# Inverse in tiles of 32 rows, attention scores of two heads together, and new rates for the work beside them

## The chip, the cores and the metric

The program runs on one core of one Trainium2 chip. The metric is the device time of one execution in microseconds (us); three executions of the kernel before took 1747.9, 1748.63 and 1761.38 us, median 1748.63.

A core has a matrix engine (TensorE, PE in the profile; its weight loads are PEld), VectorE (DVE), ScalarE (ACT), GpSimd (POOL) and SyncE (SP), which here issues DMA transfers. The engines run side by side, each through its own list of instructions in order, and wait for each other by semaphores. SBUF is the on-chip memory with 128 partitions, PSUM the small memory into which TensorE writes.

## The reference

All arrays are fp32, 256 tokens (T) of 1024 features (D). Two blocks run one after the other:

- `first_block`: two layers of attention with an mLSTM branch, each followed by a convolutional feed-forward network (FFN, 2816 wide).
- `second_block`: one layer. A mixer of three branches, each of which reads the tokens ("lat") and a second sequence of 256 context tokens ("ctx"): HGRN2, RWKV-7 and neighbourhood attention. Then a mixture of 32 experts, all of whose weights are read.

The change touches two of the branches. RWKV-7 is a recurrence over tokens, run forwards and backwards, for 4 heads of 64, first over ctx and then over lat:

```
def step(s, inp):
    r_t, w_t, k_t, v_t, kk_t, ak_t = inp
    sa = jnp.einsum('bhvk,bhk->bhv', s, kk_t)
    s = s * w_t[:, :, None, :] - sa[..., None] * ak_t[:, :, None, :] + v_t[..., None] * k_t[:, :, None, :]
    return s, jnp.einsum('bhvk,bhk->bhv', s, r_t)
```

The kernel does 64 tokens at once, and for that has to invert one unit triangular 64x64 matrix for each chunk of 64 tokens, head and direction. Neighbourhood attention (8 heads of 64) scores each token against the window of 4 rows by 16 columns around it, with a bias by relative place, and against all 256 context tokens, under one softmax:

```
s_win = jnp.where(in_win[:, :, None, :], s_win + bias, NEG_INF)
s_ctx = jnp.einsum('bhjqd,bhld->bhjql', q_row, kc_h) * scale
```

## The kernel before, in words

**Projections.** The state x stays in SBUF, features on partitions. Weights are streamed: `load` (L442) issues a DMA on SP into a `raw` tile; `split_w` makes two tiles of it, `hi` by a copy on ACT (L451) and `lo` by a subtraction on DVE (L453). Each product is three matmuls: `mm3` (L474 to L476, 256 tokens wide) or `mm3n` (L487 to L489, tokens as weights).

**Order of the work.** Code is written as Python generators. `background(gen, rate)` adds one to a list, and each `tick()` of the code in front adds `rate` to each entry's account and runs one step per whole number. So a rate of 0.6 means three steps in five ticks. From what is so recorded a scheduler makes each engine's list; the lists below show the result.

**RWKV-7.** `rwkv(rp, j, m, lat)` (L1296) treats two heads (j) and runs four times: the two ctx runs as background steps (rate 0.8) inside the two FFNs, about 345 to 430 us and 800 to 880 us, the two lat runs in `middle()`, about 1075 to 1245 us. One run is a preparation (from L1307: decay, keys `kt`, `at`, `kr`, five transposes by L644, the products L1402), then the inverse, then the steps over chunks. The inverse takes eight units side by side (4 chunks by 2 heads), each as two 64x64 matrices, one for each direction, on the two halves of the 128 partitions. It grows X = inverse of blocks of 2, 4, ... 64 rows in six levels (L1427). Level 0 is elementwise. At each of the other five, `bt` is the part of the matrix that joins two blocks (DVE, L1429); `products` (L1424) computes bt*X into PSUM with 16 matmuls 64x64; ACT copies it to y (L1436); `products` computes X*y; DVE subtracts it from X (L1439); DVE transposes X into XT in squares of 32 (L1440). At the last level XT itself is updated (L1443). A product waits for the copy or the transpose before it, so in PE's list other matmuls stand between.

**Neighbourhood attention.** `scores(hd)` (L1750), one head at a time: a DMA of the bias, 128x384 (L1754); a mask added to it on POOL (L1755); for each half of the queries (128 tokens) two matmuls of 256 columns into one PSUM buffer "d", window and context (L1759). Their 64 features lie on partitions 0 to 63 for even heads and 64 to 127 for odd ones. DVE adds the bias (L1763), ACT copies the context part (L1765), then come maximum, exponential, four transposes (L644) and the product with the values (L1786). Scores run two pieces ahead.

**`middle()`** (L1823) runs the mixer of the tokens: HGRN2 (`hg`) in front, with `rwkv_lat` (`rk`) beside it at 0.6; after that `na_inputs`, the projections of neighbourhood attention; then neighbourhood attention with the rest of `rk`, whose rate stays at 0.6. PSUM has two buffers "d", three "a", two "y", one "f". The expert stage begins at about 1313 us: 32 experts, whose weights (L2079, L2097) come by DMA straight into the matmuls.

Of the kernel before, what the change touches and what calls it, by code (L numbers as in the profile page):

```python
# [15 lines left out]
AF = mybir.ActivationFunctionType  # L16
OP = mybir.AluOpType
AX = mybir.AxisListType
PSUM = bass.MemoryType.PSUM
P = 128  # L20
T = 256
NEG = -1.0e30
# [14 lines left out]
ADA_RATE, RK_RATE, MID_RATES = (0.8, 0.45, 0.8, 0.45), 0.8, (0.6, 1.0, 1.0, 1.0, 0.6)  # L37
# [143 lines left out]
def _consts2():  # L181

    c = Vecs()
    t = np.arange(P)

    q = np.arange(T)
# [9 lines left out]
    k, c = c, Vecs()  # L196
    c.add("tri", np.concatenate([t[:, None] > t[None, :], t[:, None] < t[None, :]], axis=1))
    r, c = c, Vecs()
# [11 lines left out]
    for b in (1, 2, 4, 8, 16, 32):  # L210
        same = s // (2 * b) == u // (2 * b)
        lev.append(par(same & (s // b < u // b), same & (s // b > u // b)).reshape(P, -1))
    c.add("rklev", np.concatenate(lev, axis=1))
    c.add("eye2", np.tile(np.eye(64), (2, 1)))
    n, c = c, Vecs()

    qc, kc = t[:, None] % 64, np.arange(64)[None, :]
    w0 = np.clip(qc - 8, 0, 48)
    c.add("nawin", np.where((kc >= w0) & (kc < w0 + 16), 0.0, NEG))
    return k, r, e, n, c  # L220


def prep(inputs):
# [78 lines left out]
    a["rpb"] = np.stack(b).reshape(P, -1)  # L302
# [7 lines left out]
    for group, k in zip(("all", "one", "two", "tri", "moe", "rk", "na"), (*_consts(), *_consts2())):  # L310
        a["k_" + group] = k.array()
        cat.update({n: (group, *x) for n, x in k.at.items()})
# [39 lines left out]
class Net:  # L352
# [943 lines left out]
    def rwkv(self, rp, j, m, lat):  # L1296
# [117 lines left out]
        X, XT = ti([8, 64], "kt"), ti([8, 64], "at")  # L1414
# [3 lines left out]
        f3 = lambda t: t.rearrange("p (s c) -> p s c", s=8)  # L1418
        units = [(g, p, slice(64 * p, 64 * p + 64)) for g in range(8) for p in range(2)]

        def products(tag, l_, r_):
            ps = self.ps(tag)
            for g, p, r in units:
                nc.tensor.matmul(ps[r, g * 64 : g * 64 + 64], l_(g, p, r), r_(g, p, r), start=True, stop=True, skip_group_check=True)  # L1424
            return ps

        for l in range(6):  # L1427
            bt = ti([8, 64], "bt", 2)
            nc.vector.tensor_tensor(f2(bt), f2(AT), lev[:, l, :].unsqueeze(1).to_broadcast([P, 4, P]), OP.mult)  # L1429
            if l == 0:  # L1430
                nc.vector.scalar_tensor_tensor(XT, bt, -1.0, self.C("eye2").unsqueeze(1).to_broadcast([P, 8, 64]), OP.mult, OP.add)
                nc.vector.transpose(f1(X), f1(XT))
                continue
            ps = products("a", lambda g, p, r: bt[r, g, :], lambda g, p, r: X[r, g, :])
            y = ti([8, 64], "y1")
            nc.scalar.copy(f1(y), ps)  # L1436
            if l < 5:
                ps = products("a", lambda g, p, r: XT[r, g, :], lambda g, p, r: y[r, g, :])
                nc.vector.tensor_tensor(X, X, f3(ps), OP.subtract)  # L1439
                nc.vector.transpose(f1(XT), f1(X))  # L1440
            else:
                ps = products("a", lambda g, p, r: y[r, g, :], lambda g, p, r: XT[r, g, :])
                nc.vector.tensor_tensor(XT, XT, f3(ps), OP.subtract)  # L1443
            yield

# [299 lines left out]
    def neighbourhood(self, np_, m):  # L1745
# [4 lines left out]
        def scores(hd):  # L1750

            hs = slice(64 * (hd % 2), 64 * (hd % 2) + 64)
            bias = self.two("twoa").rearrange("p a t -> p (a t)")[:, :384].rearrange("p (x c) -> p x c", c=64)
            nc.sync.dma_start(bias, self.A["rpb"][:, hd * 384 : hd * 384 + 384].rearrange("p (x c) -> p x c", c=64))  # L1754
            nc.gpsimd.tensor_tensor(bias, bias, self.C("nawin").unsqueeze(1).to_broadcast([P, 6, 64]), OP.add)  # L1755
            for i in range(2):
                ps = self.ps("d")
                for n, k in enumerate((kl[hd // 2][hs], self.naK[hs, hd // 2, :])):
                    nc.tensor.matmul(ps[:, n * T : n * T + T], q[hd // 2][hs, i * P : i * P + P], k, start=True, stop=True,  # L1759
                                     skip_group_check=True)  # L1760
                s = self.tmp(512, "nas")
                b0 = 2 * (1 - i)
                nc.vector.tensor_tensor(s[:, :T].rearrange("p (r c) -> p r c", c=64), ps[:, :T].rearrange("p (r c) -> p r c", c=64),  # L1763
                                        bias[:, b0 : b0 + 4, :], OP.add)
                nc.scalar.copy(s[:, T:], ps[:, T:])  # L1765
                mx = self.tmp(1, "namx", bufs=4)
                nc.vector.tensor_reduce(mx, s, AX.X, OP.max)
                nc.vector.tensor_scalar(mx, mx, -1.0, None, OP.mult)
                nc.scalar.activation(s, s, AF.Exp, bias=mx, accum_out=den[:, i, hd : hd + 1])
                yield s  # L1770

        todo = [(hd, i) for hd in range(8) for i in range(2)]
        ready = (s for hd in range(8) for s in scores(hd))
# [49 lines left out]
    def middle(self):  # L1823
        nc, x = self.nc, self.x
        self.ew = {"ew0": self.ectx.enter_context(self.pool("ew0"))}
        with self.pool("yp") as yp, self.pool("mid") as mp, self.phase("s", {256: 3, 512: MID_BUFS}):
# [6 lines left out]
            self.consts("na", mp)  # L1833
# [18 lines left out]
            while na in self.bg:  # L1852
                self.tick()
            self.background(self.prefetch(5), OUT_RATES[2])
# [341 lines left out]
```

## Time and profile before

| what | value |
|---|---|
| executions | 1747.9, 1748.63, 1761.38 us |
| the profiled execution | 1758.49 us; span 1756.4 us |
| PE, DVE, ACT, POOL busy, share of the span | 90%, 64%, 43%, 4% |
| DMA, mean over the span | 262 GB/s |
| expert stage, 1313 to 1756 us | 443 us, DMA at 408 GB/s |

The profiled execution is 9.9 us above the median of the three. Shares of busy time are averages over stages with different limits. A "record" is one matmul instruction in the trace; each fp32 matmul of the inverse and of the scores leaves two records. `PE L1424 ... x32` in a timeline is a run of 32 records of one kind without another between: its start, and the time from the first's start to the last's end. A matmul's record is longer than the distance to the next one, since they are pipelined, so a run's cost is the distance of starts. "PEclk" is TensorE's granted clock, 1.00 for 2.4 GHz and 0.50 for 1.2 GHz.

### The profile page before, as it was taken

How to read it: one execution, taken by the hardware profiler on the slowest of the kernel's cores; microseconds unless marked ns; L12 is line 12 of the kernel's file. 1: busy time of each engine (PE TensorE's matmuls, PEld its weight loads, DVE VectorE, ACT ScalarE, POOL GpSimd, SP SyncE). 2: the span in 40 equal slices, each digit the busy share in tenths (PEclk: the TensorE clock that was granted, in tenths of full speed). 3: DMA queues.
4: the chain of work that ended last, by engine and by line, in shares of the span. 5: the costliest groups of instructions: out<-in, count | busy, mean ns of one | idle time of the engine just before them, and what ended most of it. 6: DMA issues, size and time to landing. Idle time of an engine off the chain costs nothing.

```text
span 1756.4 us, 32561 instructions
## 1 busy us (share of the span) xinstructions
PE 1576.2 (90%) x13542; PEld 1271.6 (72%) x13542; DVE 1118.8 (64%) x2155; ACT 758.8 (43%) x1259; POOL 72.8 (4%) x77
## 2 busy tenths in 40 slices
PE   4999999999998999999999999999989777776776
PEld 4898999899997899989999899878874312221211
DVE  7989868898897887789889878666652111111011
ACT  3576545764455754556455576553431000000000
POOL 0000000020010000001011001001000000000000
PEclk8899999999999999999999999989989888988878
DMA  9745765666675467466567733223459999999998
GB/s 392 310 159 209 262 246 192 223 216 236 226 263 190 179 247 281 172 230 239 194 224 259 281 138 132 74 76 138 195 212 419 419 416 416 417 417 418 419 416 343
DMA packets 76809, 460.81 MB, mean 262 GB/s; under 512 B 8562, under 2 KB 11122, under 8 KB 28146
## 3 DMA queue, kind: packets, MB, share of 16 engines
q1 hardware_dynamic: 74352, 452.45, 67.1%
q10 hardware_dynamic: 2306, 6.24, 1.0%
q8 instruction: 108, 1.77, 0.4%
q14 instruction: 43, 0.35, 0.1%
HBM read 457.61 MB, written 1.05 MB: 261 GB/s over the span
## 4 chain that ended last, share of the span: by engine, by line
PE 57%; DMA 24%; DVE 12%; ACT 4%; issue 3%; SPq 0%; POOL 0%; DVEq 0%; ACTq 0%; POOLq 0%
DMA ew<-in_wgu 11%; PE d L474 9%; PE d L476 9%; PE d L475 9%; DMA ew<-in_wdown 8%; DVE lo L453 4%; PE y L474 3%; PE y L476 3%; PE y L475 3%; PE a L1424 3%; DVE raw L537 3%; PE d L2079 2%; DMA raw<-in_ws 2%; PE a L2008 1%; ACT hi L451 1%
## 5 line engine op out<-in xcount | busy, mean ns | idle before, releaser
L451 ACT CAST hi<-raw 128x1024 fp32r<-128x1024 f32 x309 | 322.7, 1048 | 295.6 <-PE d L475 173.1
L453 DVE TENSOR_TENSOR lo<-raw,hi 128x1024 fp32r<-128x1024 f32 x309 | 379.9, 1236 | 86.2 <-ACT hi L451 84.8
L474 PE MATMUL d<-hhi,hi 128*128 128x256 f32 x1320 | 387.4, 295 | 13.7 <-ACT hhi L608 10.4
L475 PE MATMUL d<-hlo,hi 128*128 128x256 f32 x1320 | 382.4, 290 | 3.7 <-DVE hlo L611 3.2
L476 PE MATMUL d<-hhi,lo 128*128 128x256 f32 x1320 | 381.4, 289 | 2.4 <-DVE lo L453 2.4
L474 PEld LDWEIGHTS d<-hhi,hi 128*128 128x128 f32 x1320 | 258.4, 196 | 22.1 <-ACT hhi L608 13.4
L475 PEld LDWEIGHTS d<-hlo,hi 128*128 128x128 f32 x1320 | 259.6, 197 | 7.4 <-DVE hlo L611 5.0
L476 PEld LDWEIGHTS d<-hhi,lo 128*128 128x128 f32 x1320 | 259.8, 197 | 4.5 <-DVE lo L453 3.2
L2079 PE MATMUL d<-ew,xe 128*32 128x512 f32 x984 | 167.2, 723 | 53.2 <-DMA ew<-in_wgu 52.8
L537 DVE SCALAR_TENSOR_TENSOR raw<-raw,cb 128x1024 f32<-128x1024 f32 x160 | 195.1, 1232 | 4.7 <-DMA raw<-in_ada 4.3
L2079 PEld LDWEIGHTS d<-ew,xe 128*32 128x32 f32 x984 | 27.0, 117 | 166.8 <-DMA ew<-in_wgu 140.1
L2084 DVE SCALAR_TENSOR_TENSOR moa<-moa,d 128x512 f32<-128x512 f32 x8 | 5.5, 688 | 177.1 <-ACT moa L2083 177.1
L474 PE MATMUL y<-hhi,hi 128*128 128x256 f32 x352 | 100.9, 287 | 0.0
L476 PE MATMUL y<-hhi,lo 128*128 128x256 f32 x352 | 99.9, 284 | 0.0
L475 PE MATMUL y<-hlo,hi 128*128 128x256 f32 x352 | 99.6, 283 | 0.0
L2097 PE MATMUL y<-ew,mht 128*32 128x512 f32 x472 | 70.5, 649 | 31.6 <-DMA ew<-in_wdown 27.3
L2115 DVE SCALAR_TENSOR_TENSOR x<-f,mod_l,x 128x256 f32<-128x256 f32 x32 | 14.0, 479 | 129.6 <-PE f L2111 129.6
L459 POOL TENSOR_TENSOR hidl<-fgel,hidh 128x256 fp32r<-128x256 f32 x44 | 52.6, 1196 | 829.6 <-ACT hidh L458 786.9
L2083 ACT ACTIVATE moa<-d 128x512 f32<-128x512 f32 x8 | 4.8, 597 | 183.4 <-PE d L2079 183.4
L2097 PEld LDWEIGHTS y<-ew,mht 128*32 128x32 f32 x472 | 12.5, 114 | 79.5 <-DMA ew<-in_wdown 60.5
L474 PEld LDWEIGHTS y<-hhi,hi 128*128 128x128 f32 x352 | 67.4, 192 | 0.6
L476 PEld LDWEIGHTS y<-hhi,lo 128*128 128x128 f32 x352 | 67.4, 192 | 0.3
(669 smaller groups left out, 3180.4 us busy)
## 6 DMA issues: line engine op xcount, KB each, us to landing
raw<-in_ws SPq DMA_DIRECT2D x151, 1024.0 KB, 4.9
ew<-in_wgu SPq DMA_DIRECT2D x100, 1024.0 KB, 18.0
raw<-in_ada SPq DMA_DIRECT2D x80, 1024.0 KB, 5.0
ew<-in_wdown SPq DMA_DIRECT2D x46, 1024.0 KB, 19.8
ew<-in_wgu SPq DMA_DIRECT2D x46, 512.0 KB, 13.8
ew<-in_wdown SPq DMA_DIRECT2D x28, 512.0 KB, 12.6
two<-in_wgu SPq DMA_DIRECT2D x20, 256.0 KB, 8.4
two<-in_wdown SPq DMA_DIRECT2D x16, 256.0 KB, 7.9
```

The lines of the kernel that those rows point to most:

```text
L451: f.append(nc.scalar.copy(hi_, raw))
L453: f.append(nc.vector.tensor_tensor(lo_, raw, hi_.bitcast(F32), OP.subtract))
L459: (eng or self.nc.vector).tensor_tensor(lo, src, hi.bitcast(F32), OP.subtract)
L474: nc.tensor.matmul(out, whi, hhi, start=first and i == 0, stop=False, **s)
L475: nc.tensor.matmul(out, whi, hlo, start=False, stop=False, **s)
L476: nc.tensor.matmul(out, wlo, hhi, start=False, stop=last and i == n - 1, **s)
L537: self.nc.vector.scalar_tensor_tensor(w, w, 0.5, c, OP.mult, OP.mult, accum_out=out)
L1424: nc.tensor.matmul(ps[r, g * 64 : g * 64 + 64], l_(g, p, r), r_(g, p, r), start=True, stop=True, skip_group_check=True)
L2008: nc.tensor.matmul(ps[:, k * P : k * P + P], xn[:, i, d : d + P], of(i), start=i == 0, stop=i == 1, skip_group_check=True)
L2079: nc.tensor.matmul(ps[32 * e : 32 * e + 32, :], xe[:, k, 32 * e : 32 * e + 32], w[e], start=k == 0, stop=k == 7, skip_group_check=True)
L2097: nc.tensor.matmul(py[q][32 * e : 32 * e + 32, :], ht[:, f * P + 32 * e : f * P + 32 * e + 32], w[e], start=f == 0, stop=f == 3, skip_grou ...
L2115: nc.vector.scalar_tensor_tensor(x[:, j, :], ps[:, c * T : c * T + T], g2[:, j : j + 1], x[:, j, :], OP.mult, OP.add)
```

## The change

Three things. First, the inverse keeps only the diagonal 32x32 squares of X until the last level, in tiles of 8 x 32 columns instead of 8 x 64; a product is 32 matmuls of 32x32 (four on the four quarters of the partitions, eight times) instead of 16 of 64x64, and copy, subtraction and transpose have 256 columns instead of 512. Level 0 needs four DVE instructions instead of one. The last level fills the off-diagonal quarter: four copies on ACT and four on DVE for one subtraction on DVE.

Second, `scores(hp, i)` takes the two heads of a pair for one half of the queries: one DMA of 128x2x256 (8 in all, as before), no mask on POOL (the mask is in the bias table), and two PSUM buffers "d", whose matmuls alternate between the lower and the upper 64 partitions.

Third, the rates of `rk`: 0.9 beside HGRN2 (was 0.6), 0.25 beside `na_inputs` (was 0.6), 0.9 beside neighbourhood attention (was 0.6).

```diff
-ADA_RATE, RK_RATE, MID_RATES = (0.8, 0.45, 0.8, 0.45), 0.8, (0.6, 1.0, 1.0, 1.0, 0.6)
+ADA_RATE, RK_RATE, MID_RATES = (0.8, 0.45, 0.8, 0.45), 0.8, (0.9, 1.0, 1.0, 1.0, 0.25, 0.9)
...
-        X, XT = ti([8, 64], "kt"), ti([8, 64], "at")
+        xx, XW = ti([2, 8, 32], "kt"), ti([8, 64], "at")
+        X, XT = xx[:, 0], xx[:, 1]
...
+        quads = [(g, q % 2, slice(32 * q, 32 * q + 32)) for g in range(8) for q in range(4)]
+        half = lambda a: slice(32 * a, 32 * a + 32)
...
+        def products32(l_, r_, other=False):
+
+            ps = self.ps("a")
+            for g, a, r in quads:
+                o = r if not other else slice(r.start + 32 - 64 * a, r.stop + 32 - 64 * a)
+                nc.tensor.matmul(ps[o, g * 32 : g * 32 + 32], l_(g, a, r), r_(g, r), start=True, stop=True, skip_group_check=True)
+            return ps[:, :T].rearrange("p (g c) -> p g c", g=8)
+
         for l in range(6):
             bt = ti([8, 64], "bt", 2)
             nc.vector.tensor_tensor(f2(bt), f2(AT), lev[:, l, :].unsqueeze(1).to_broadcast([P, 4, P]), OP.mult)
             if l == 0:
-                nc.vector.scalar_tensor_tensor(XT, bt, -1.0, self.C("eye2").unsqueeze(1).to_broadcast([P, 8, 64]), OP.mult, OP.add)
+                for q in range(4):
+                    r, c = slice(32 * q, 32 * q + 32), half(q % 2)
+                    nc.vector.scalar_tensor_tensor(XT[r], bt[r, :, c], -1.0, self.C("eye2")[r, c].unsqueeze(1).to_broadcast([32, 8, 32]),
+                                                   OP.mult, OP.add)
                 nc.vector.transpose(f1(X), f1(XT))
                 continue
-            ps = products("a", lambda g, p, r: bt[r, g, :], lambda g, p, r: X[r, g, :])
-            y = ti([8, 64], "y1")
-            nc.scalar.copy(f1(y), ps)
-            if l < 5:
-                ps = products("a", lambda g, p, r: XT[r, g, :], lambda g, p, r: y[r, g, :])
-                nc.vector.tensor_tensor(X, X, f3(ps), OP.subtract)
+            last = l == 5
+            ps = products32(lambda g, a, r: bt[r, g, half(a ^ last)], lambda g, r: X[r, g, :], last)
+            y = ti([8, 64], "y1").rearrange("p (x g) c -> p x (g c)", x=2)[:, 0].rearrange("p (g c) -> p g c", g=8)
+            nc.scalar.copy(y, ps)
+            if not last:
+                ps = products32(lambda g, a, r: XT[r, g, :], lambda g, r: y[r, g, :])
+                nc.vector.tensor_tensor(X, X, ps, OP.subtract)
                 nc.vector.transpose(f1(XT), f1(X))
             else:
-                ps = products("a", lambda g, p, r: y[r, g, :], lambda g, p, r: XT[r, g, :])
-                nc.vector.tensor_tensor(XT, XT, f3(ps), OP.subtract)
+                ps = products32(lambda g, a, r: y[r, g, :], lambda g, r: XT[r, g, :], True)
+                for q in range(4):
+                    r, a = slice(32 * q, 32 * q + 32), q % 2
+                    nc.scalar.copy(XW[r, :, half(a)], XT[r])
+                    nc.vector.tensor_copy(XW[r, :, half(1 - a)], ps[r])
             yield
+        XT = XW
...
-        def scores(hd):
-
-            hs = slice(64 * (hd % 2), 64 * (hd % 2) + 64)
-            bias = self.two("twoa").rearrange("p a t -> p (a t)")[:, :384].rearrange("p (x c) -> p x c", c=64)
-            nc.sync.dma_start(bias, self.A["rpb"][:, hd * 384 : hd * 384 + 384].rearrange("p (x c) -> p x c", c=64))
-            nc.gpsimd.tensor_tensor(bias, bias, self.C("nawin").unsqueeze(1).to_broadcast([P, 6, 64]), OP.add)
-            for i in range(2):
-                ps = self.ps("d")
-                for n, k in enumerate((kl[hd // 2][hs], self.naK[hs, hd // 2, :])):
-                    nc.tensor.matmul(ps[:, n * T : n * T + T], q[hd // 2][hs, i * P : i * P + P], k, start=True, stop=True,
+        def scores(hp, i):
+
+            bias = self.two("twoa")
+            nc.sync.dma_start(bias, self.A["rpb"][:, 768 * hp : 768 * hp + 768].rearrange("p (h c) -> p h c", h=2)[:, :, P - i * P : P - i * P + T])
+            pss = [self.ps("d") for _ in range(2)]
+            for n, k in enumerate((kl[hp], self.naK[:, hp, :])):
+                for ps, r in zip(pss, (slice(0, 64), slice(64, P))):
+                    nc.tensor.matmul(ps[:, n * T : n * T + T], q[hp][r, i * P : i * P + P], k[r], start=True, stop=True,
                                      skip_group_check=True)
+            for h2, ps in enumerate(pss):
                 s = self.tmp(512, "nas")
-                b0 = 2 * (1 - i)
-                nc.vector.tensor_tensor(s[:, :T].rearrange("p (r c) -> p r c", c=64), ps[:, :T].rearrange("p (r c) -> p r c", c=64),
-                                        bias[:, b0 : b0 + 4, :], OP.add)
+                nc.vector.tensor_tensor(s[:, :T], ps[:, :T], bias[:, h2, :], OP.add)
...
-        todo = [(hd, i) for hd in range(8) for i in range(2)]
-        ready = (s for hd in range(8) for s in scores(hd))
+        todo = [(2 * hp + h2, i) for hp in range(4) for i in range(2) for h2 in range(2)]
+        ready = (s for hp in range(4) for i in range(2) for s in scores(hp, i))
...
             while na in self.bg:
                 self.tick()
+            rk[1] = MID_RATES[5]
```

Three places in PE's list show what moves. In the list of the changed kernel all lines up to 1410 are lower by one (L474 is L473, L644 is L643, L1340 is L1339, L1402 is L1401), L1424 of the inverse is L1433, and L1759 is L1774.

**The preparation of the second lat run, before.** PE's list from the last product for the rates (L1340, out of `ma`) through the transposes (L644) to the first product L1402; `kr`, `kt`, `at` are tiles that DVE writes from decay and rates, `mv` is ready long before:

```order
L489 MATMUL d_13987<-hi_14054,hlo_11862 128x256
L1340 MATMUL a_13910<-ma_12105,up_13861 128x256
L644 MATMUL a_13956<-kon_339,mv_1861_12777 128x128 x2
L644 MATMUL a_13960<-kon_339,kr_13894 128x128 x2
L1151 MATMUL y_13974<-two_13972,kon_339 128x512
L644 MATMUL a_14000<-kon_339,kt_13895 128x128 x4
L644 MATMUL a_14018<-kon_339,at_13896 128x128 x4
L1402 MATMUL a_14033<-kr_13894,kt_13895 64x128
```

Nothing of the projections stands between the transposes of `mv`, `kr`, `kt` and `at`.

**The same place now.** From the first transpose of `mv` to that of `kr` (cut where the projection's three lines repeat):

```order
L643 MATMUL a_14392<-kon_339,mv_1840_12983 128x128 x2
L473 MATMUL d_14277<-hhi_12201,hi_14368 128x256
L474 MATMUL d_14277<-hlo_12202,hi_14368 128x256
...
L1732 MATMUL y_14327<-hsq_14325,kon_339 128x512
L473 MATMUL d_14421<-hhi_12201,hi_14424 128x256
...
L643 MATMUL a_14396<-kon_339,kr_14297 128x128 x2
L473 MATMUL d_14421<-hhi_12201,hi_14424 128x256
...
L643 MATMUL a_14446<-kon_339,kt_14298 128x128 x3
```

Between the transposes of `mv` and of `kr` there are now 25 matmuls (24 of the projection and L1732), before `kt` six more; the two products L1340 stand 15 and 3 matmuls ahead of that of `mv`.

**Products and scores.** PE's list where the inverse of the second lat run meets the scores, before:

```order
L1759 MATMUL d_14417<-y4lo_12565,y4hi_12562 128x256
L1424 MATMUL a_14130<-y_2064_14128,at_14104 64x64 x16
L1759 MATMUL d_14417<-naK,y4hi_12562 128x256
L1759 MATMUL d_14427<-y4lo_12565,y4hi_12562 128x256
L1424 MATMUL a_14166<-kt_14103,bt_14164 64x64 x16
L1759 MATMUL d_14427<-naK,y4hi_12562 128x256
```

and now:

```order
L1774 MATMUL d_14906<-y4lo_13031,y4hi_13028 128x256
L1433 MATMUL a_14784<-y_2073_14782,kt_14638 32x32 x32
L1774 MATMUL d_14907<-y4lo_13031,y4hi_13028 128x256
L1774 MATMUL d_14906<-naK,y4hi_13028 128x256
L1433 MATMUL a_14829<-kt_14638,bt_14827 32x32 x32
L1774 MATMUL d_14907<-naK,y4hi_13028 128x256
L1433 MATMUL a_14864<-y_2077_14862,kt_14638 32x32 x32
L1774 MATMUL d_14928<-y4lo_13031,y4hi_13028 128x256
L1774 MATMUL d_14928<-naK,y4hi_13028 128x256
```

The two heads' matmuls (d_14906 and d_14907) seldom stand side by side: products come between them.

## Rows read from the trace of the kernel before

**Rows 1.** The page, first part: busy us, share of the span, instructions.

```profile
PE 1576.2 (90%) x13542; PEld 1271.6 (72%) x13542; DVE 1118.8 (64%) x2155; ACT 758.8 (43%) x1259; POOL 72.8 (4%) x77
```

**Rows 2.** Windows (from:to, us, busy by engine, PEclk, DMA share, GB/s).

```profile
374.00:385.00 11.00, 11.00 (x137) 10.60 (x136) 10.90 (x21) 6.83 (x13) 2.70 (x2) 1.00 0.75 270
...
858.00:869.00 11.00, 11.00 (x138) 10.61 (x137) 7.95 (x13) 3.73 (x4) 0.00 (x0) 1.00 0.64 247
...
1172.00:1176.00 4.00, 2.16 (x8) 0.87 (x8) 3.71 (x8) 3.71 (x9) 0.00 (x0) 1.00 0.00 0
1176.00:1180.00 4.00, 3.49 (x15) 2.39 (x16) 3.26 (x7) 3.17 (x6) 0.00 (x0) 0.54 0.02 6
...
1188.00:1192.00 4.00, 4.00 (x22) 3.82 (x19) 3.30 (x5) 0.37 (x1) 1.42 (x1) 0.50 0.60 231
...
1196.00:1220.00 24.00, 23.89 (x419) 19.84 (x419) 14.68 (x29) 10.89 (x25) 1.99 (x2) 1.00 0.46 171
...
1313.00:1756.00 443.00, 335.24 (x1987) 107.81 (x1986) 57.30 (x133) 35.47 (x73) 0.00 (x0) 0.87 1.00 408
```

**Rows 3.** Waits of 341 to 500 us: who for whom, us, times, longest.

```profile
ACT hi L451 <- PE d L475: 30.0, 18, 3.6
```

**Rows 4.** PE's timeline at a product: start, us, engine, line, tile, records.

```profile
378.59 0.28 PE L475 MATMUL y<-hlo,hi 128*128 128x256 f32 x1
378.71 0.28 PE L476 MATMUL y<-hhi,lo 128*128 128x256 f32 x1
378.92 1.15 PE L1424 MATMUL a<-kt,bt 64*64 64x64 f32 x32
379.99 0.39 PE L474 MATMUL y<-hhi,hi 128*128 128x256 f32 x1
```

**Rows 5.** Groups by line: records, ns of one (least/median/most), first and last.

```profile
L1424 PE MATMUL a<-kt,bt x640: 216/218/267, 378.9 to 1217.3; 64*64 64x64 f32 x160
...
L1436 ACT COPY y<-a x20: 565/586/590, 380.3 to 1217.6; 128x512 f32<-128x512 f32 x20
...
L1439 DVE TENSOR_TENSOR kt<-kt,a x16: 669/686/689, 382.8 to 1214.9; 128x512 f32<-128x512 f32 x16
...
L1763 DVE TENSOR_TENSOR nas<-d,two x16: 408/424/425, 1200.2 to 1280.1; 128x256 f32<-128x256 f32 x16
```

**Rows 6.** PE's timeline elsewhere: runs of other widths and tiles.

```profile
1090.56 1.09 PE L1402 MATMUL a<-kr,kt 64*64 64x128 f32 x16
1091.48 0.92 PE L1402 MATMUL a<-kr,at 64*64 64x128 f32 x13
...
1160.02 0.36 PE L1494 MATMUL a<-NT,vn 64*64 64x64 f32 x8
1160.19 0.32 PE L1495 MATMUL a<-RA,sa 64*64 64x64 f32 x8
...
1298.75 0.61 PE L1922 MATMUL a<-wr,x 128*128 128x36 f32 x4
1299.20 0.58 PE L1925 MATMUL a<-ones,two 128*128 128x1 f32 x4
```

**Rows 7.** PE's timeline, second lat run's preparation; brackets: idle time and its releaser.

```profile
1174.82 0.44 PE L644 MATMUL a<-kon,kr 128*128 128x128 f32 x2 [1.84 <-DVE kr L1360]
...
1176.62 1.12 PE L644 MATMUL a<-kon,kt 128*128 128x128 f32 x4 [0.51 <-DVE kt L1356]
```

**Rows 8.** PE's timeline, scores between products.

```profile
1197.68 0.70 PE L1759 MATMUL d<-y4lo,y4hi 64*128 64x256 f32 x2
1198.31 1.15 PE L1424 MATMUL a<-y,at 64*64 64x64 f32 x32
...
1201.52 0.48 PE L1759 MATMUL d<-naK,y4hi 64*128 64x256 f32 x1
...
1202.33 0.86 PE L1424 MATMUL a<-y,at 64*64 64x64 f32 x22
```

**Rows 9.** Who waited for the products L1424, whole span (us, times).

```profile
  ACT y L1436: 15.3, 12
```

More of the change, by code (lines that the diff above doesn't have):

```diff
@@ L211, in _consts2 @@
         same = s // (2 * b) == u // (2 * b)
-        lev.append(par(same & (s // b < u // b), same & (s // b > u // b)).reshape(P, -1))
+        lev.append(par(same & (s // b < u // b), same & (s // b > u // b)).reshape(P, -1) * (1.0 if b < 32 else -1.0))
     c.add("rklev", np.concatenate(lev, axis=1))
     c.add("eye2", np.tile(np.eye(64), (2, 1)))
[L215 to L220, printed above, removed]
+    return k, r, e, c
 def prep(inputs):
@@ L301, in prep @@
     b = [np.lib.stride_tricks.as_strided(rp[:, 5 - par :, 63:], (64, 8, 6, 64), (-st[2], st[0], st[1], st[2])) for par in (0, 1)]
-    a["rpb"] = np.stack(b).reshape(P, -1)
+    qc, kc = np.arange(64)[:, None], np.arange(64)[None, :]
+    w0 = np.clip(qc - 8, 0, 48)
+    win = ((kc >= w0) & (kc < w0 + 16))[None, :, None, None, :]
+    a["rpb"] = np.where(win, np.stack(b), np.float32(NEG)).astype(np.float32).reshape(P, -1)
     a["wr"] = np.concatenate([g["w_router_group"][0], g["w_router_expert"][0]], axis=1).reshape(8, P, 36).transpose(1, 0, 2).reshape(P, -1)
@@ L309, in prep @@
     cat = {}
-    for group, k in zip(("all", "one", "two", "tri", "moe", "rk", "na"), (*_consts(), *_consts2())):
+    for group, k in zip(("all", "one", "two", "tri", "moe", "rk"), (*_consts(), *_consts2())):
         a["k_" + group] = k.array()
@@ L1417, in rwkv @@
         f1 = lambda t: t.rearrange("p s c -> p (s c)")
-        f3 = lambda t: t.rearrange("p (s c) -> p s c", s=8)
         units = [(g, p, slice(64 * p, 64 * p + 64)) for g in range(8) for p in range(2)]
+        quads = [(g, q % 2, slice(32 * q, 32 * q + 32)) for g in range(8) for q in range(4)]
+        half = lambda a: slice(32 * a, 32 * a + 32)
         def products(tag, l_, r_):
@@ L1768, in scores @@
                 nc.vector.tensor_scalar(mx, mx, -1.0, None, OP.mult)
-                nc.scalar.activation(s, s, AF.Exp, bias=mx, accum_out=den[:, i, hd : hd + 1])
+                nc.scalar.activation(s, s, AF.Exp, bias=mx, accum_out=den[:, i, 2 * hp + h2 : 2 * hp + h2 + 1])
                 yield s
-        todo = [(hd, i) for hd in range(8) for i in range(2)]
-        ready = (s for hd in range(8) for s in scores(hd))
+        todo = [(2 * hp + h2, i) for hp in range(4) for i in range(2) for h2 in range(2)]
+        ready = (s for hp in range(4) for i in range(2) for s in scores(hp, i))
         s = [next(ready) for _ in range(NA_AHEAD)]
@@ L1832, in middle @@
             self.dump("x1", x)
-            self.consts("na", mp)
             late = self.ew["ew0"].tile([P, 2048], F32, tag="late", bufs=1, name=self.uid("late"))
```

## The prediction

> **What bounds the kernel now.** First the page's busy times: PE is busy for 90% of the span [rows 1], so the question is where it is not, and whether a matmul saved is time saved. The windows answer it by stage. In the FFNs and in most of `middle()` PE is busy for the whole window: 11.00 of 11 us in both FFN windows, 23.89 of 24 us from 1196 to 1220 us [rows 2]. The waits of the first FFN say the same: ACT stands still for PE (30.0 us in 18 waits, for the PSUM or weight tiles that PE has not yet released) [rows 3]. So before 1313 us a product taken off PE shortens the kernel, but DVE is close behind: 10.90 of 11 us in the window of 374 us, 7.95 in that of 858 us [rows 2]. From 1313 us on the DMA share is 1.00 for 443 us [rows 2]. That stage has its own length, and shifts as a whole: what is gained before it arrives at the end.
>
> The one large hole is at 1172 to 1176 us: PE is busy for 2.16 of 4 us [rows 2]. PE's timeline names the cause: the transposes of `kr` wait 1.84 us, those of `kt` 0.51 us, both for DVE [rows 7]. Right after it the granted clock is 0.54, and it is 0.50 in the window of 1188 us still, with PE busy throughout [rows 2].
>
> **The change, part by part.** All sums are made against the profiled execution, 1758.5 us; what that is on the scale of the median comes after them.
>
> *The products.* One costs 1.16 us of PE's path: L474 would have followed L476 after 0.12 us, as L476 follows L475, so at 378.83; it starts at 379.99 [rows 4]. Of this, first start to last start is the run's 1.15 less the last record's 0.22 us [rows 4, 5]: 0.93 us, 58 ns for each of 16 slots of two records. The other 0.23 us goes with entering and leaving, and stays. With 32 rows there are twice as many matmuls, 64 records. If the four quarters of the partitions run side by side, these are again 16 slots, of 32 columns and not 64. No row shows a 32x32 tile. The nearest: with 128 columns a slot takes 0.92/8 = 115 ns (L1402) [rows 6], twice the 58 ns of 64 columns, so the line through both gives 30 ns at 32. That four tiles run at once the rows of L1494 and L1495 show: 16 records from 1160.02 us to the next matmul at 1160.43; less 0.23 that is 0.18 us, 11 ns each where a product has 29 [rows 6, 4]. Four starts of 11 ns are 45 ns. I take 33 ns, near the line, since those 11 ns were reached with 64 columns in each and are no limit on starts; that is 0.53 us and a gain of 0.40 a product. The ends: 30 ns (gain 0.45) and 58 ns (gain nothing); worse than that is a rival. There are 20 copies L1436 [rows 5], one for each two products: 40 products, half in the FFNs, half in `middle()`. So 8.0 us there and 8.0 us here. In the FFNs I keep back 1 us, as DVE leaves PE at some places only 0.1 us in 11. In `middle()` three products are now cut in two by other matmuls: 3 x 0.2 us back. **-7.0 and -7.4 us.**
>
> *DVE and ACT of the inverse.* Half as wide, subtraction and transpose go from 0.69 to about 0.42 us (the 256-wide L1763) [rows 5]: 4 levels x 2 x 0.26 = 2.1 us less of DVE in a run. Level 0 and the last level have four instructions for one: 4 x 0.42 - 0.69 = 1.0 us more each. The sum is nothing, on an engine that PE outlasts. The copies y are shorter; four more copies on ACT, at most 0.59 us each [rows 5], lie on an engine that waits for PE. **0.**
>
> *Scores.* One matmul alone between products costs 0.63 us (1197.68 to 1198.31), two of different halves of the partitions together 0.81 us (1201.52 to 1202.33) [rows 8]: 0.45 us saved for a pair that stands together. All 16 would give 7.2 us; in the new list products stand between most, and I count four or five: **-2.0 us**, with ends 0 and 7.2. The POOL masks go; POOL is busy 4% [rows 1] and PE does not wait for it. DMAs: eight before and after, a third larger each; SP queues them behind weight loads, in a stretch where the bias is read two pieces ahead. 0.
>
> *The rates.* The preparation now stands between 24 projection matmuls before `kr` and six before `kt`, so DVE has their time: 24 x 0.12 [rows 4] = 2.9 us against waits of 1.84 and 0.51 us [rows 7]. These 2.35 us go, and with the hole the lower clock: four windows, 1176 to 1192 us, at 0.54 to 0.50 [rows 2], 16 us with half of full-speed work in them: 7.8 us lost. Together 10.2 us; I take **-8.0**, since some of those windows are small dependent steps. Ends 0 and -10.2. What is late next: the inverse runs beside the scores with shorter products, so the cover of each copy or transpose is shorter too. Before, ACT waited for products 15.3 us, not PE for ACT [rows 9]. A cover of one score matmul (0.63 us) stands against about 0.4 us of copy, or 0.84 of subtraction and transpose, plus the product's own drain of 0.22. I add 0.3 us at eight places: **+2.5 us**, with ends 0 and 6; the upper end also has the merged projections queue on PE behind a score pair that holds both buffers "d".
>
> Sum: -7.0 - 7.4 - 2.0 - 8.0 + 2.5 = -21.9, so 1736.6 us on the scale of the profiled execution. That execution is 9.9 us above the median. If the others are lower in everything alike, the median becomes 1726.7; if the lower clock after the hole is what they lack, 8 us are not theirs to gain, and it is 1748.6 - 13.9 = 1734.7. I take 1730 between.
>
> **The rivals.**
>
> *A. The products gain nothing (0.18).* Four matmuls of 36 columns take 1299.20 - 1298.75 = 0.45 us, 112 ns a record, and a run of four with one column is as long (0.58 to 0.61 us) [rows 6]: below some width a record gets no shorter. Those have 128x128 weights, and the 64x64 tiles go down to 58 ns, so I think the floor goes with the width of the weights; if it doesn't, 32 columns cost what 64 do, and all else is left: -7.5 us, about 1742. The Trainium skill, page "TensorEngine Tiling (Array Packing)", section Performance Considerations, has such a floor: some 60 cycles of overhead for each matmul, so that one column takes as long as 60; it advises against tiling a dimension that is already small. The two runs of rows 6 agree that there is one. By that rule 32 columns would cost as 60, and the estimate from that page is a gain near nothing too.
>
> *B. Slower: the tiles run in twos (0.08).* If only two of the four quarters overlap, 64 records come at the present 29 ns: 1.86 us for 0.93, +37 us in 40 products, less 7.5: +29.7 us, 1788 on the profiled scale, about 1780 on the median's. It decides at 0.93 + 7.5/40 = 1.12 us a product. For it: no 32-row tile is in the trace; L1424 now shows two side by side. Against: L1494 and L1495.
>
> *C. The hole moves (0.12).* The same DVE chain stops PE elsewhere, or the lower clock comes with the sparser work after it. Then only the 14 us of the products and scores are left, less another 2 to 6 us of waits: about 1738.
>
> **How the numbers follow.** Forecast 0.58, A 0.18, B 0.08, C 0.12; 0.04 for new waits above 8 us that leave it unchanged or slower. Downwards the ends are -2 for the products, -2.2 for the stall, -5.2 for the scores and -2.5 with no new waits; together 11.9, which hardly fall all at once, but from 1726.7 they reach 1715, and I set 1713. Upwards the range has to take in A and C, with some waits: 1747. Outside lie B and the rest. One per cent, 17.5 us, is about what can be told from no change: faster means below 1731.1. The forecast lies at the edge: 0.72 of its chance counts as faster, a quarter of C's, a little of A's: 0.46. Slower: B and some of the rest, 0.10. Same: 0.44.
>
> **What would show it.** The runs of L1433: 64 records in 0.53 us from the first start to the last if the forecast holds, 0.93 in A, 1.86 in B. No idle time of PE before the transposes of `kr` and `kt`, and a granted clock of 1.00 through the projections after it; otherwise C. The two heads' scores together 0.81 us. The first L2079 some 20 us earlier than 1313, with 443 us after it; if that stage grows, the gain is given back to the DMA. The forecast is wrong if PE is no longer full in the FFN windows, with DVE full in its place.

## The result, and the profile after

The changed kernel takes 1764.56 us (median of 18 executions, 1759.64 to 1772.7) against 1748.93 us (18 executions, 1743.92 to 1761.38): ratio 1.0079, 95% interval 1.0062 to 1.0096. It is slower by 0.8%, where 1730 us were forecast and 1747 us was the upper end of the range. The ratios here and below are taken over all executions and not from the two medians (which give 1.0089), without executions that count as slow, of which there are two, in e9 (1770.04 and 1771.51 us). The profiled execution is one of 1768.98 us, with a span of 1767.2 us. Its page has the busy times and, in the third part, the DMA queues (packets, MB, share):

```profile
PE 1578.8 (89%) x14822; PEld 1263.9 (72%) x14822; DVE 1120.2 (63%) x2183; ACT 757.5 (43%) x1271; POOL 62.7 (4%) x69
...
q8 instruction: 118, 1.93, 0.4%
```

The same line of the queue in the page of before:

```profile
q8 instruction: 108, 1.77, 0.4%
```

PE has 1280 matmuls and as many weight loads more than in [rows 1]: 40 products with 32 more of each. The queue q8 has 10 packets more, of 16 KB each (1.93 MB in 118). So 2560 instructions are 10 packets: q8 brings PE's program (its code), 256 instructions to a packet. The experiments below bear it out: each page with 14182 matmul records has 113 packets, half of the difference. This column of the page is the one that the prediction did not read.

The product itself is as forecast. PE's timeline of the changed kernel, one product in the first FFN and one wait soon after it:

```profile
379.99 0.28 PE L475 MATMUL y<-hhi,lo 128*128 128x256 f32 x1
380.20 0.75 PE L1433 MATMUL a<-kt,bt 32*32 32x32 f32 x64
380.88 0.38 PE L473 MATMUL y<-hhi,hi 128*128 128x256 f32 x1
...
382.12 0.39 PE L475 MATMUL y<-hhi,lo 128*128 128x256 f32 x1 [0.45 <-DVE lo L452]
```

Counted as in [rows 4], a product costs 380.88 - 380.11 = 0.77 us of PE's path, where it was 1.16: 0.39 us less. The wait for `lo` is new: DVE is the limit there now and then, as the window of the same stretch shows (before, PE was busy for 11.00 of these 11 us [rows 2]):

```profile
374.00:385.00 11.00, 10.55 (x200) 9.89 (x199) 10.81 (x22) 6.75 (x12) 2.04 (x2) 1.00 0.57 194
```

The expert stage begins at 1323.6 us instead of 1313 and is as long as in [rows 2] (443.6 us). In these two profiles all that is lost is lost in `middle()`. PE's timeline there, the two longest of the new waits:

```profile
1101.14 0.75 PE L1433 MATMUL a<-y,kt 32*32 32x32 f32 x64
1101.82 0.80 PE L1635 MATMUL f<-hsm,hg 64*64 64x64 f32 x20
1104.64 0.45 PE L1635 MATMUL f<-hsm,hg 64*64 64x64 f32 x8 [2.02 <-issue]
...
1199.11 0.75 PE L1433 MATMUL a<-kt,bt 32*32 32x32 f32 x64
1199.79 0.70 PE L1774 MATMUL d<-naK,y4hi 64*128 64x256 f32 x2
1200.65 0.34 PE L1433 MATMUL a<-y,kt 32*32 32x32 f32 x18 [0.16 <-DVE kt L1453]
1204.40 0.86 PE L1433 MATMUL a<-y,kt 32*32 32x32 f32 x46 [3.41 <-issue]
1205.18 1.22 PE L1774 MATMUL d<-y4lo,y4hi 64*128 64x256 f32 x2
```

Both waits stand in the middle of a run of equal matmuls, which wait for no other engine ("issue"): 46 of the 64 records of a product come 3.41 us after the first 18. The windows there (from:to, us, busy time of PE, PEld, DVE, ACT, POOL with instructions, PEclk, DMA share, GB/s):

```profile
1190.00:1200.00 10.00, 9.77 (x364) 8.32 (x363) 8.16 (x14) 3.63 (x8) 0.00 (x0) 1.00 0.59 209
1200.00:1210.00 10.00, 6.43 (x118) 4.46 (x118) 4.84 (x13) 2.14 (x6) 0.00 (x0) 0.71 0.62 232
1210.00:1220.00 10.00, 10.00 (x115) 7.13 (x114) 2.86 (x9) 3.65 (x11) 0.00 (x0) 0.50 0.11 34
1220.00:1230.00 10.00, 10.00 (x159) 8.24 (x160) 3.61 (x8) 3.60 (x9) 0.00 (x0) 0.50 0.12 29
```

From 1190 to 1200 us PE goes through 727 instructions, 73 a us; before, in [rows 2], 1196 to 1220 us, it was 838 in 24 us, 35 a us. Then it stands, and the granted clock is 0.50 for the next 20 us and more. Those 35 are an average over 24 us; the densest ten microseconds of the kernel before, and a dense stretch of the change that has no long wait, are these windows:

before:

```profile
1110.00:1120.00 10.00, 10.00 (x243) 9.10 (x241) 7.55 (x15) 6.08 (x14) 1.33 (x2) 1.00 0.29 107
```

the change:

```profile
1110.00:1120.00 10.00, 10.00 (x333) 7.92 (x334) 7.69 (x16) 7.54 (x17) 1.09 (x2) 0.90 0.01 3
```

So the kernel before reached 48 instructions a us, and in the change 67 a us still went with PE busy all the time, there with the DMA engines idle (share 0.01).

The queue q8 in two narrow windows of the same trace (packets, MB, share of the engines in that window):

1190 to 1200 us:

```profile
q8 instruction: 1, 0.02, 0.6%
```

1202 to 1203 us, the first packet after it:

```profile
q8 instruction: 1, 0.02, 5.8%
```

One packet of 256 instructions came in ten microseconds in which 727 were spent; PE stops at 1201.0, the next packet is on its way at 1202, and PE goes on at 1204.40. From 1102 to 1110 us, around the other wait, three packets come, one in about 3.4 us.

The trace has one more sign that these are waits for code. Count PE's instructions from the start, with its semaphore instructions: it stands after 20161 and after 23489 of them. Both numbers are 193 more than a multiple of 256, so both waits fall on the same place of a packet. The long waits of e1 and e6 below do so too (193 or 194), and each of these six ends 1.40 to 1.48 us after the transfer of a packet of q8 has ended.

Why the packet comes so late is not shown in full. The ones that end the two waits begin 4.8 and 6.6 us after the packet before, although one can come in 3.4. Just before, other transfers, mostly weights, take most of the DMA engines' time; their queue, q1, has this share of all 16 from 1099 to 1102 us and from 1199 to 1202 us:

```profile
q1 hardware_dynamic: 124, 0.93, 77.0%
q1 hardware_dynamic: 159, 1.17, 93.8%
```

No run has the same code with these transfers moved away, so how much of a wait is theirs stays open.

The Trainium skill, page "Runtime: NRT & Kernel Launch", section Instruction fetch mechanics, says that an engine streams its program in blocks of 256 instructions through a DMA queue of its own, and that this is mostly hidden. The block's size agrees with these rows; that it is hidden does not hold here.

### The profile page after: what moved, and what is told of

It reads as the page before. It is cut to its first block, busy times and chain, and to the rows that moved or that the text cites. A ratio compares the mean times of both kernels' runs of the same rounds, so it can differ in the third digit from the quotient of the medians.

```text
span 1767.2 us, 35137 instructions
## 1 busy us (share of the span) xinstructions
PE 1578.8 (89%) x14822; PEld 1263.9 (72%) x14822; DVE 1120.2 (63%) x2183; ACT 757.5 (43%) x1271; POOL 62.7 (4%) x69
## 3 DMA queue, kind: packets, MB, share of 16 engines
q8 instruction: 118, 1.93, 0.4%
## 5 line engine op out<-in xcount | busy, mean ns | idle before, releaser
L473 PE MATMUL d<-hhi,hi 128*128 128x256 f32 x1320 | 388.2, 295 | 14.4 <-ACT hhi L607 10.2
L474 PE MATMUL d<-hlo,hi 128*128 128x256 f32 x1320 | 382.8, 290 | 3.9 <-DVE hlo L610 3.6
L473 PEld LDWEIGHTS d<-hhi,hi 128*128 128x128 f32 x1320 | 258.3, 196 | 23.8 <-ACT hhi L607 13.0
L474 PEld LDWEIGHTS d<-hlo,hi 128*128 128x128 f32 x1320 | 259.9, 197 | 8.3 <-DVE hlo L610 5.6
L473 PE MATMUL y<-hhi,hi 128*128 128x256 f32 x352 | 101.0, 287 | 0.0
L474 PE MATMUL y<-hlo,hi 128*128 128x256 f32 x352 | 99.7, 283 | 0.0
L2111 PE MATMUL y<-ew,mht 128*32 128x512 f32 x472 | 76.2, 703 | 25.3 <-DMA ew<-in_wdown 20.9
L473 PEld LDWEIGHTS y<-hhi,hi 128*128 128x128 f32 x352 | 67.4, 192 | 1.6 <-issue 1.1
```

Source lines behind the costliest of these rows:

```text
L473: nc.tensor.matmul(out, whi, hhi, start=first and i == 0, stop=False, **s)
L474: nc.tensor.matmul(out, whi, hlo, start=False, stop=False, **s)
L2111: nc.tensor.matmul(py[q][32 * e : 32 * e + 32, :], ht[:, f * P + 32 * e : f * P + 32 * e + 32], w[e], start=f == 0, stop=f == 3, skip_grou ...
```

## The experiments

Theory 1 (code): PE runs out of code where the 32-row products stand dense; the waits and the half clock after them cost more than the products gain. Rivals: the rates pack the steps too densely (theory 2), the score pairs block PSUM (theory 3), the steps between products are too short a cover for copy and transpose (theory 4).

**e1: the inverse alone** (rates and scores of before; shown against the change).

```diff
-ADA_RATE, ... MID_RATES = ... (0.9, 1.0, 1.0, 1.0, 0.25, 0.9)
+ADA_RATE, ... MID_RATES = ... (0.6, 1.0, 1.0, 1.0, 0.6)
-        def scores(hp, i):
+        def scores(hd):
```

> The 32-row inverse alone, scores and rates as before. Theory 1 (code): PE's instructions come in transfers of 16 KB, about 256 PE rows each (load or matmul); a product has 128 rows now in 0.56 us where it had 64 in 0.93, and where products and HGRN2's own small matmuls stand dense PE runs out of code, stands 2 to 3 us for nothing that the profile shows, and the clock falls to half after it. Then the 16 us of the products come back in part: between 1742 and 1756 us, with waits named issue of 2 us or more before L1433 or its neighbours, and a half-clock stretch after each. Theory 2 (rates): the loss is of the rates, which pack the chain of steps; then the inverse alone gains its 13 us: 1733 to 1738, with no such waits.

1758.3 us against 1750.37, ratio 1.0043 (1.0021 to 1.0066): 2 us over the interval of theory 1, and far from that of theory 2. PE's timeline has a code wait right behind a product (from 1115 to 1118 us the DMA share is 0.92 here too):

```profile
1116.36 0.65 PE L1434 MATMUL a<-kt,bt 32*32 32x32 f32 x52
1116.95 0.66 PE L644 MATMUL y<-kon,hvg 128*128 128x128 f32 x4
1117.54 0.75 PE L1434 MATMUL a<-y,kt 32*32 32x32 f32 x64
1120.87 0.39 PE L475 MATMUL d<-hlo,hi 128*128 128x256 f32 x1 [2.57 <-issue]
```

**e2: the rates alone.**

```diff
+ADA_RATE, ... MID_RATES = ... (0.9, 1.0, 1.0, 1.0, 0.25, 0.9)
+            rk[1] = MID_RATES[5]
```

> The new rates alone, 64-row inverse and single scores. Theory 1: no code waits over 1 us, the hole before the transposes of kr is gone and its half-clock stretch with it: 1738 to 1746 us. Theory 2: DVE-bound holes at 1050 to 1070 and 1150 to 1170 us and a half-clock stretch elsewhere, 1752 to 1764 us.

1750.63 us, ratio 0.9993 (0.997 to 1.0015): no difference. Both theories missed; the rates neither harm nor help. PE's waits between 1040 and 1295 us (who for whom, us, times, longest):

```profile
PE y L1602 <- DVE hd L1600: 1.4, 1, 1.4
PE a L1402 <- ACT nat L1379: 0.9, 1, 0.9
PE a L1424 <- DVE nas L1763: 0.7, 1, 0.7
PE a L1424 <- DVE kt L1439: 0.7, 2, 0.5
```

The wait for `kt` of [rows 7] is gone and that for `kr` down to 0.2 us, as planned, and these have come: the first in HGRN2 (rate 0.9 puts more of DVE's work before it), the second one step further in the same preparation. Both stand at 1.4 and 0.9 us in all eight profiles with the new rates, and in the six with the old ones there is no wait for `hd` and at most 0.2 us for `nat`.

**e3: the paired scores alone.** The edit is the hunk of `scores` in the change.

> The paired scores alone, old inverse and rates. Theories 1 and 2: 1744 to 1749 us. Theory 3 (a pair takes both buffers d, and the merged projections and na_inputs wait behind it): 1752 to 1760 us.

1757.62 us, ratio 1.0028 (1.0001 to 1.0055), the twelve executions spread from 1746.64 to 1765.48. The median lies in the interval of theory 3 and not in that of theories 1 and 2. But no wait for a buffer "d" is over 0.5 us in its trace, and together with the rates (e4) nothing of a loss is left. So the mechanism of theory 3 has no support, and why the scores alone are this slow stays open.

**e4: the change with the 64-row inverse.**

```diff
-        xx, XW = ti([2, 8, 32], "kt"), ti([8, 64], "at")
+        X, XT = ti([8, 64], "kt"), ti([8, 64], "at")
... (and the rest of the inverse as before)
```

> The change with the 64-row inverse put back: new rates and paired scores. Theory 1: the code waits of 2.0 and 3.4 us at 1103 and 1201 us and the half clock after them are gone, and all that is left is a gain: 1736 to 1746 us. Theory 2: the rates do the harm, so it stays at 1755 to 1768 us.

1751.22 us, ratio 0.9995 (0.9973 to 1.0017). The code waits are gone, as theory 1 had it, and theory 2 falls; but 5 us above its interval: rates and scores together gain nothing. So all of the loss belongs to the inverse, when it stands beside them (13.3 us from e4 to the change; alone, in e1, it loses 8).

**e5: half the code in the lat runs.**

```diff
             for g, a, r in quads:
+                if g % step:
+                    continue
-                nc.tensor.matmul(ps[o, g * 32 : g * 32 + 32], l_(g, a, r), r_(g, r), ...)
+                nc.tensor.matmul(ps[o, g * 32 : g * 32 + 32 * step], l_(g, a, r), r_(g, r), ...)
```

with `step = 2 if lat else 1`, and two groups' columns in `r_`. It leaves out every second group of weights, so half of the inverse is wrong: the run serves for its time alone.

> The whole change, but in the two lat runs each product has 16 matmuls of 32x64 instead of 32 of 32x32: every second group of weights is left out and its columns are moved through its neighbour's, so half of the inverse is not what it should be. TensorE's time for a product stays (8 slots of 58 ns for 16 of about 33), its code halves, and every copy, transpose and wait stays. Theory 1 (code): no waits named issue over 1 us in middle, no half-clock stretch at 1105 or 1204 us, and 1744 to 1752 us. Theory 4 (the steps between the products are too short a cover for copy and transpose): nothing changes, 1760 to 1768 us.

1738.83 us (six executions, 1735.48 to 1740.69) against 1748.70 for before beside e5 to e8, ratio 0.9939 (0.9915 to 0.9963): 25.7 us below the change, 5 us better than theory 1 said. A product in its timeline, and its waits named issue (line 1438, whole span):

```profile
1177.89 0.65 PE L1438 MATMUL a<-y,kt 32*32 32x64 f32 x32
```

```profile
  issue: 1.7, 4
```

TensorE's time of a product is near that of the change (0.65 for 0.75 us; 0.10 us less, 2 us in the 20 products), the copies, transposes and their order are the same; the number of instructions is halved. Theory 4 is refuted for the change: with the same covers there is nothing of the loss. In ten microseconds of this profile 656 instructions go through without a wait, though the DMA share is 0.34:

```profile
1089.50:1099.50 10.00, 10.00 (x328) 8.42 (x328) 8.88 (x21) 4.53 (x11) 1.38 (x3) 1.00 0.34 111
```

From 1040 to 1300 us this profile has 17 us of half clock, that of the change 48.

**e6: the same code, twice the columns, in the lat runs.**

```diff
-                nc.tensor.matmul(ps[o, g * 32 : g * 32 + 32], l_(g, a, r), r_(g, r), ...)
+                rr = r_(g, r)
+                w = rr.shape[-1]
+                nc.tensor.matmul(ps[o, g * wd : g * wd + w], l_(g, a, r), rr, ...)
```

with `wd = 64 if lat else 32`.

> The whole change, but in the two lat runs each of the 32 matmuls moves 64 columns and not 32 (the second 32, those of the next group, are not used). Code and waits as in the change, PE's time of a product back to about 0.93 us, 20 products, +7.5 us of PE. Theory 1 (code): a product's 128 rows are then spent over 1.1 us and not 0.6, so the code waits become shorter by what PE's work grows: within 4 us of the change, 1761 to 1768 us. Theory 4: PE's longer products come on top, 1770 to 1774 us.

1759.54 us, ratio 1.0061 (1.0037 to 1.0086): 1.5 us below the interval of theory 1 and 10 below that of theory 4. A product takes 0.98 us from its start to the next matmul's here, 0.68 in the change, so 20 products have 6 us more of TensorE's work (7.5 were expected); still the kernel is not slower than the change. That it is 5 us faster by the medians is within the two intervals. The same places in PE's timeline:

```profile
1191.24 1.05 PE L1438 MATMUL a<-kt,bt 32*32 32x64 f32 x64
...
1194.88 0.71 PE L1438 MATMUL a<-y,kt 32*32 32x64 f32 x40 [0.95 <-issue]
...
1200.82 1.43 PE L1438 MATMUL a<-y,kt 32*32 32x64 f32 x50 [1.96 <-issue]
```

The long wait, after the same 23489 instructions of PE, is 1.96 instead of 3.41 us: slower products give the code time to come. This speaks for theory 1 and against theory 4.

**e7: the 32-row inverse in the FFNs only**, all else as in the change.

```diff
+        if not lat:
             xx, XW = ti([2, 8, 32], "kt"), ti([8, 64], "at")
...
+        else:
+            X, XT = ti([8, 64], "kt"), ti([8, 64], "at")
```

> The whole change, but 64-row products in the two lat runs: the 32-row inverse only in the FFNs, where each product stands among 256-column matmuls with two PE rows per 0.12 us. Theory 1: no code wait anywhere; against the kernel with the 64-row inverse throughout (1751.2 us) a gain of 10 x 0.37 us in each FFN less what DVE takes back: 1744 to 1749 us. Theory 4: DVE and ACT limit the FFNs as well, no gain: 1749 to 1755 us.

1746.57 us, ratio 0.9982 (0.9961 to 1.0003); in the interval of theory 1, with no code wait in its trace. It is 4.7 us below e4 by the medians and 2 by the ratios, whose intervals overlap. Against the change, 18.0 us less: that is what the 32-row inverse costs in the lat runs.

**e8: the same alone**, in the kernel before.

> The kernel before with the 32-row inverse in the two ctx runs alone; scores, rates and the lat runs as before. Theory 1: 4 to 7 us faster than before, ratio 0.996 to 0.998, with the same two groups of times as before. Theory 4: no difference, 0.999 to 1.001.

1745.54 us, ratio 0.9986 (0.9966 to 1.0006). It lies between what theory 1 said (0.996 to 0.998) and theory 4 (0.999 to 1.001), and its interval reaches into both; e7 and e8 are no clear gain over before each by itself.

**e9: 64x64 weights, 32 columns, in the lat runs**: an exact way to half the code.

```diff
+                nc.tensor.matmul(ps[r, g * 32 : g * 32 + 32], l_[r, g, :], r_[r, g, :], ...)
...
+                nc.vector.tensor_tensor(y.rearrange("p g (x c) -> p g x c", x=2), ps.unsqueeze(2).to_broadcast([P, 8, 2, 32]),
+                                        bd.unsqueeze(1).to_broadcast([P, 8, 2, 32]), OP.mult)
```

> The whole change, but the lat runs' products have 16 matmuls with 64x64 weights and 32 columns: block-diagonal weights (bt as it is; y spread over both halves by one DVE multiplication with a mask of 512 columns instead of the ACT copy), X and XT compact as in the change. Code rows as in the 64-row inverse, half its columns, one DVE step 0.3 us longer on the chain of each level. The inverse is exact again. Theory 1 (code): no waits named issue over 1 us. If a slot of 32 columns then takes 33 ns in spite of 64 columns of weights: 1738 to 1743 us, as e5_half_the_rows. If the 64 columns of weights hold the slot at 58 ns: 1746 to 1752 us, as e7_ffn_inverse_and_rest or a little worse. Theory 4 (cover of the steps): 1752 to 1760 us, since the chain is longer than in the change.

**e10: the same in the kernel before.**

> The same inverse (32-row tiles in the FFNs, 64x64 weights with 32 columns in the lat runs) in the kernel before: rates 0.6 and single scores as before. 3 us above or below e9_64_rows_32_columns, with a part of the runs some 8 us longer where the hole before the transposes of kr and the lower clock after it come.

e9: 1760.64 us, ratio 1.0036 (1.0008 to 1.0065), with executions from 1741.99 to 1771.51, before beside them 1750.52; e10: 1752.82 us, ratio 1.0016 (0.9991 to 1.004). Both missed: e9's median lies above all three of its intervals, nearest to that of theory 4 (1752 to 1760), and e10 is 8 us below e9 where 3 were said, though two of its twelve executions are some 8 us longer than the rest, as said. Neither is the better version that was hoped for. PE's timeline of e9 shows why nothing is gained:

```profile
1187.79 1.12 PE L1435 MATMUL a<-kt,y 64*64 64x32 f32 x32
1188.85 0.66 PE L646 MATMUL f<-kon,nas 128*128 128x128 f32 x4
```

Half the columns, and 1.06 us from start to start where [rows 4] have 1.07: with 64x64 weights a slot stays near 58 ns (1.12 less the last record's 0.22 is 0.90 us, 56 ns for each of 16).

**e11 and e12: a second profile of the kernel before, and of e9.**

> The kernel before once more, for a second profile. Its executions fall into two groups, about 1744 to 1751 and 1755 to 1763 us; the profile that the prediction was made from is of the upper one. If the half-clock stretch of 17 us after the hole is what parts them, an execution of about 1748 us has the hole at the transposes of kr as well, but 3 or 4 us of half clock after it instead of 17. If not, the stretch is there in either group.

> e9_64_rows_32_columns once more, for a profile of one of its long executions (ten of twelve were 1756 us or more, the profiled one 1742.6). If half-clock stretches part them: one or more stretches of 7 to 30 us between 1040 and 1300 us that the first profile has not, after a wait of PE of 1 us or less, and no wait named issue. If code does: waits named issue of 2 us or more.

e11 took 1745.67 us. PE's wait for `kr` is the one of [rows 7], but of the lower clock little is left (windows, then the wait):

```profile
1170.00:1174.00 4.00, 2.16 (x8) 0.86 (x7) 3.88 (x8) 3.70 (x9) 0.00 (x0) 0.86 0.00 0
1174.00:1178.00 4.00, 4.00 (x29) 2.92 (x28) 3.09 (x7) 3.53 (x7) 0.00 (x0) 0.71 0.02 6
1178.00:1194.00 16.00, 15.85 (x220) 13.12 (x217) 14.44 (x26) 7.39 (x14) 1.03 (x1) 1.00 0.56 202
```

```profile
PE a L644 <- DVE kr L1360: 1.8, 1, 1.8
```

Executions of the kernel before fall into two groups: of the 35 beside e1 to e4, 23 took up to 1753 us and 12 took 1755 us or more. After the same hole the clock is low for 3.4 us in this one and for 17 us in the one that the prediction was made from (1758.49). These are one profile of each group; that the clock is what parts the groups is likely, and not shown. e12 took 1745.07 us and shows, like the first profile of e9 (1742.6), no code wait. Ten of e9's twelve executions were 1756 us or more and none of them was profiled: what makes those long stays open, and theory 4, e9's longer chain on DVE, is not excluded there.

## Why the prediction was wrong, point by point

**The products, in time: right.** 0.39 us less on PE's path for 0.40 forecast. Rivals A and B fell. The floor follows the size of the weights, as argued: 32x32 tiles take 0.56/16 = 35 ns a slot, 64x64 weights with 32 columns stay near 58 (e9). Whether the rows or the columns of the weights decide was not parted. The rule of the Trainium skill, page "TensorEngine Tiling (Array Packing)", section Performance Considerations, that below some 60 columns a matmul gets no shorter, holds in e9 and not for the 32x32 tiles: 64 records in 0.56 us.

**The products, in the sum: here it failed.** In the FFNs, 7.0 us were forecast; e7 against e4 has 4.7 by the medians and 2 by the ratios, not clear of the spread. The profiles agree with a gain of about half: from the first matmul on `kt` in the first FFN to the last on `hidl` in the second it is 659.9 to 663.3 us in the five profiles with the 64-row inverse there and 654.4 to 661.2 in the nine with 32 rows, on average 3.7 us less. The 1 us held back for DVE was too little.

In `middle()` -7.4 us were forecast. Where the code is halved, e5 against e7, it is 1738.83 - 1746.57 = -7.7 us; that this is so near is in part luck, since e5's products save 0.50 us each (0.58 us from the first start to the next matmul's, where it was 1.08), 10 us in all. With the code as it is, 1764.56 - 1746.57 = +18.0 us. The step that failed is the one that said "64 records" and costed them by TensorE alone: 128 instructions in 0.56 us had to be brought as well, half a packet for each product. The code therefore costs 1764.56 - 1738.83 = 25.7 us, less some 2 us for e5's shorter products. An estimate from the two profiles finds most of it: 2.02 and 3.41 us of waiting, and 31 us more of half clock in the change than in e5, worth at most half of that, 15 us; together 21. 34 of the change's 48 us of half clock follow these two waits. None of the prediction's rivals was this; only its 0.04 for new waits above 8 us held what came.

**The stall: mis-sized.** -8.0 us were taken for the rates, out of 7.8 for the clock and 2.35 for the waits; e2 has a ratio of 0.9993, no difference. The hole was filled, but 3.7 us of smaller waits came (e2's rows), and the long half-clock stretch was not in the second profile of the kernel before (e11). The prediction saw that it might not be in the median, and still took most of it.

**The scores: no gain found**, for -2.0 forecast; e3 is rather slower, and e4 has no gain. Where two heads' matmuls do stand together they take 0.63 us (1198.47 to 1199.11 in the change), less than the 0.81 forecast, but products stand between most.

**New waits: +2.5 us for too short covers.** The waits came, but not for copies and transposes: in the change, L1433 waits 0.8 us for `kt` between 1040 and 1300 us and 5.6 us for code, together with L1635. **Rival C** said that the hole moves and lower clock with it. That happened, for the most part by another cause: C had 2 to 6 us of waits, the code cost 25.7. C itself is there in small too: the change waits for `nat` in the same preparation, and the clock is 0.66 in the window after it (3.4 us of full-speed work lost in those 10):

```profile
1168.96 0.87 PE L1401 MATMUL a<-kr,kt 64*64 64x128 f32 x10 [0.94 <-ACT nat L1378]
```

```profile
1170.00:1180.00 10.00, 10.00 (x56) 8.20 (x56) 6.50 (x8) 4.72 (x7) 0.00 (x0) 0.66 0.81 283
```

It was given 0.12 and 1738 us.

## What to carry to other kernels

Count instructions beside TensorE's time: smaller tiles that double the matmuls double the code as well, and where PE would spend its program faster than it had been spent before (here 73 instructions a us, where the densest ten microseconds had 48), look at the queue that brings it, at waits named "issue" in the middle of a run of equal matmuls, at what else fills the DMA engines there, and at the clock after them. The same tiles lose where they stand among other small ones, and do no harm where they stand among long matmuls (e7, e8; their gain there is not clear of the spread). A price read from one profile has to be held against the spread of the executions.

## What the runs showed of the hardware that was not expected

PE's program comes in packets of 16 KB, 256 instructions, and in a dense stretch of the change one came in about 3.4 us; PE stood 2.0 to 3.4 us where it outran them, each time at the same place of a packet. After the 3.41 us wait the granted clock was 0.50 from 1204 to 1231 us with PE busy 10.00 of 10 us; in e6, after 1.96 us, it was low for 3.4 us; after a wait of 1.8 us it was low for 17 us in one execution of a kernel and for 3.4 in another.
